# Where a mixer's small products accumulate: the projections' two PSUM banks, or first the weighed values' two

## The chip, the cores and the metric

One core of a Trainium2 chip runs the whole program. The metric is the device time of one execution in microseconds (us), the median of several runs. The core has a matrix engine (TensorE, PE in the profile, with its weight loads as PEld), a vector engine (DVE), a scalar engine (ACT), GpSimd (POOL), a queue engine for transfers (SP), and an accumulator memory (PSUM) of eight banks into which all matrix products go. Each engine takes its instructions strictly in the order in which the program holds them: an instruction that waits holds up all behind it on that engine.

## The reference

Two layers of a decoder trunk over 512 tokens and 16 meta tokens (528 positions), 1024 channels, float32. Each layer is a mixer and a feed-forward part. The mixer is what the change touches:

```python
u = rms_norm(h, pre_g)
z = jnp.einsum("bld,de->ble", u, w_in)
q, k, v, f_logit, a_val, a_gate, sc_b, sc_c, sc_x = jnp.split(z, idx, axis=-1)
...
y_attn = forgetting_attention(q, k, v, log_f)       # 8 heads of 64
a = a_val * jax.nn.sigmoid(a_gate)
a = causal_depthwise_conv(a, a_dw_w) + a_dw_b       # 31 taps, 256 channels
a = jax.nn.silu(layer_norm(a, a_ln_g, a_ln_b))
y_conv = jnp.einsum("blc,ce->ble", a, a_pw_w)       # the pointwise product
y_sc = sc_b * causal_depthwise_conv(sc_c * sc_x, sc_conv_w)
y = jnp.concatenate([y_attn, y_conv, y_sc], axis=-1)
y = jnp.einsum("ble,ed->bld", head_rms_norm(y, head_g), w_out)
return h + rms_norm(y, post_g)
```

`head_rms_norm` scales each group of 64 channels by the inverse root of its mean square. Then the feed-forward part: `w_up` to 5632 channels, a 3-tap convolution, `silu(g) * up`, `w_down`.

## The kernel before

Activations lie with channels on the 128 partitions and positions along the row, 528 of them in two halves of 264 (`H`). Every float32 product is made of three fast ones from values split into a high and a low part (`mm3`, line 671): high by high, low by high, high by low. The weights come in blocks of 128x1024; ACT rounds a block to its high part (line 625 in the planned stages), DVE subtracts for its low part (line 629).

The order of the work in a mixer is written by a planner, `Flow`. Each piece of PE work is a generator ("thread"): `fill` runs the projections one after the other, `maxima` the row maxima of each head's logits (lines 1402 and 1426), `exponentials` the logits again and their exponentials (line 1448), `weighing` the products of the exponentials with the values and their sums for a pair of heads (line 1494), `att_norms` the mean squares of a finished pair (line 1560). The convolution branch runs as `conv_tail`: the means for its layer norm (line 1578), the mean squares (line 1607), then the pointwise product; its two outputs and the two of the short convolution go through `plain_head_norm` (line 1176). The planner holds a clock for each engine with an estimated duration for each instruction, and each time it lets go on whatever could start first. What comes out of it is a fixed order of instructions on each engine; on the chip, semaphores make each instruction wait for its inputs and for its bank, whatever the planner believed.

A product may only be planned once it holds a bank. In a mixer the eight banks are four rings of two: `mm` (0, 1) for projections, `s1` (3, 4) for maxima, attention's head norms and the gate, `st` (5, 6) for logits, `acc` (2, 7) for the weighed values and their sums. A ring hands out its oldest bank, and only once the planner's clock has passed the time at which that bank's last reader ends. A projection holds a bank of `mm` through 24 matmuls and its eviction. Before the change, the layer norm's means and mean squares, the pointwise product's four halves and the plain head norms take theirs from `mm` too; so `mm` serves the projections and the convolution branch in turn. `weighing` takes both banks of `acc` and one of `s1` at once for each of the four pairs of heads.

One half of a head norm is: a matmul with `bd` on PE (the mean squares in PSUM, line 1176 or 1560), logarithm, exponential and square on ACT (lines 1141, 1144, 1145), two combining steps on DVE (1146, which reads PSUM and frees the bank, and 1149), the scaling on DVE (1160), the rounding on ACT (1163) and the low part on DVE (1164). The intermediate tiles `rs_r` and `rs_t` are two of each, so two halves can be under way at once.

When `maxima` and `fill` have ended, `Early` starts the first two columns of `w_out` on the banks of the projections: for each finished input block `k` (0 to 3 attention, 4 and 5 convolution, 6 and 7 short convolution) and half, six matmuls, in the order in which the planner expects the blocks to be normed. Those six need the block's high and low parts, the outputs of lines 1163 and 1164. So the last head norms of a mixer stand between the last projections and the rest of `w_out`.

Of the kernel before, what the change touches and what calls it, by code (L numbers as in the profile page):

```python
# [208 lines left out]
class Flow:  # L209
# [32 lines left out]
    def thread(self, gen, first=False):  # L242
        self.threads.insert(0 if first else len(self.threads), [gen, [Tok(self.pe)]])

    def grab(self, ring, slot=None):

        while True:
            t = ring.slots[0].time
            if t is not None and t <= self.pe:
                slot = slot or Slot()  # L250
                ring.take(slot)
                return slot
            yield [Head(ring)]

    @staticmethod
    def ready(waits, least=0.0):
# [56 lines left out]
def mm_us(n, k=P):  # L313

    return max(n / 2400 + 0.012, 0.00086 * k)


def act_us(n):
    return 0.17 + 0.0009 * n


def dve_us(n):
    return 0.17 + 0.00101 * n


def stt_us(n):
    return 0.22 + 0.00102 * n
# [13 lines left out]
def tile_hybrid_trunk(ctx: ExitStack, tc: tile.TileContext, xT, wflat, pv_d, out):  # L341
# [4 lines left out]
    def T(pool, shape, dt, tag, bufs=None):  # L346
        uid[0] += 1
        kw = {} if bufs is None else {"bufs": bufs}
        return pool.tile(list(shape), dt, tag=tag, name=f"{tag}_{uid[0]}", **kw)
# [18 lines left out]
    def mmt(i=None):  # L368

        if i is None:  # L370
            i = PAIRS[n_pairs[0] % 2]
            n_pairs[0] += 1
        return psum[:, i:i + 2]
# [46 lines left out]
    flow = Flow()  # L420
# [6 lines left out]
    def half_sl(hf):  # L427
        return slice(H * hf, H * (hf + 1))
# [87 lines left out]
    def act(us, fn, *after, **kw):  # L516
        return flow.op("act", us, fn, after, **kw)

    def dve(us, fn, *after, **kw):
        return flow.op("dve", us, fn, after, **kw)  # L520
# [144 lines left out]
    def mm3(dst, w, ks, rhs, start=True, stop=True, cols=slice(None)):  # L665

        n = len(ks)
        for i, k in enumerate(ks):
            for p, (a, b) in enumerate(((0, 0), (0, 1), (1, 0))):
                for hf, d in dst.items():  # L670
                    nc.tensor.matmul(d, lhsT=w[a][:, k, cols],  # L671
                                     rhs=rhs(b, k, hf),
                                     start=start and i == 0 and p == 0,
                                     stop=stop and i == n - 1 and p == 2)
# [284 lines left out]
    def mixer(l, ypool, first, close_first, spans, front, rz0_at):  # L959
        pv, pg = pvs[l]  # L960

        def col(name, j):
            return pv[:, _COLS[name] + j:_COLS[name] + j + 1]

        def gcol(name, j):
            return pg[:, _COLS[name] + j:_COLS[name] + j + 1]
# [138 lines left out]
        banks = {"mm": Ring((0, 1)), "s1": Ring((3, 4)), "st": Ring((5, 6)), "acc": Ring((2, 7))}  # L1105
        rings = {"p": Ring(NPT), "rs": Ring(2)}

        def bank(kind):

            slot = yield from flow.grab(banks[kind])  # L1110
            return psum[:, slot.buf], slot

        def proj(use):
# [16 lines left out]
        def ytiles(i):  # L1130
            return (T(ypool, [P, L], F32R, f"yhi{i}"), T(ypool, [P, L], F32R, f"ylo{i}"))
# [21 lines left out]
        def head_norm(i, yt, hf, x, slot, eps, tok):  # L1153

            if hf == 0:
                y[i] = ytiles(i)
            yhi, ylo = y[i]
            c = half_sl(hf)
            box, mine, e = rsq(x, slot, eps, tok)
            f = dve(stt_us(H), lambda: nc.vector.scalar_tensor_tensor(  # L1160
                yt[:, c], in0=yt[:, c], scalar=gcol("head_g", i), in1=box["t"], op0=ALU.mult, op1=ALU.mult), e)
            mine.close(f)
            g = act(act_us(H), lambda: nc.scalar.copy(yhi[:, c], yt[:, c]), f)  # L1163
            d = dve(dve_us(H), lambda: nc.vector.tensor_sub(ylo[:, c], yt[:, c], yhi[:, c].bitcast(F32)), g)  # L1164
            y_at[i, hf] = [g, d]
            return d

        def plain_head_norm(i, yt, sq, toks, waits=()):

            sqs = [act(act_us(H), lambda hf=hf: nc.scalar.activation(sq[:, half_sl(hf)], yt[:, half_sl(hf)], AF.Square),  # L1170
                       toks[hf], *waits) for hf in range(2)]
            out = []
            for hf in range(2):
                yield [sqs[hf]]
                ps, slot = yield from bank("mm")
                nc.tensor.matmul(ps[:, :H], lhsT=bd, rhs=sq[:, half_sl(hf)], start=True, stop=True)
                out.append(head_norm(i, yt, hf, ps[:, :H], slot, RMS_EPS, flow.mm(4 * mm_us(H))))
                yield
            return out

        def sc_norm(j):
            sq = T(mq, [P, L + 2], F32, "cxp")[:, :L]
            yield from plain_head_norm(6 + j, sc[j], sq, [sc_at[j, "b", hf] for hf in range(2)])
            sc_done[j] = True
# [381 lines left out]
        def conv_tail(blk):  # L1566

            w = blk.w
            yield taps
            a2 = [ytiles(4), ytiles(5)]  # L1570
            sq = [T(mq, [P, L + CK - 1], F32, "apad", 2) for _ in range(2)]
            us, vs = act_us(H), dve_us(H)
            at = {}
            for hf in range(2):
                c = half_sl(hf)
                ps, slot = yield from bank("mm")
                for j in range(2):
                    nc.tensor.matmul(ps[:, :H], lhsT=om_c, rhs=conv[j][:, c], start=j == 0, stop=j == 1)
                tok = flow.mm(8 * mm_us(H))
                subs = []  # L1580
                for j in range(2):
                    subs.append(dve(vs, lambda j=j, ps=ps, c=c: nc.vector.tensor_sub(
                        conv[j][:, c], conv[j][:, c], ps[:, :H]), tok))
                    at[hf, j] = act(us, lambda j=j, c=c: nc.scalar.activation(sq[j][:, c], conv[j][:, c], AF.Square), subs[-1])
                slot.close(*subs)
                yield
            done = {}

            def silu(j, c, box, mine, e):
                n, s = conv[j][:, c], sq[j][:, c]  # L1590
                f = dve(stt_us(H), lambda: nc.vector.scalar_tensor_tensor(
                    n, in0=n, scalar=gcol("a_ln_g", j), in1=box["t"], op0=ALU.mult, op1=ALU.mult), e)
                mine.use(f)
                f = dve(vs, lambda: nc.vector.tensor_scalar(n, in0=n, scalar1=col("a_ln_b", j), scalar2=None, op0=ALU.add), f)
                g = act(us, lambda: nc.scalar.activation(s, n, AF.Exp, scale=-1.0), f)
                g = act(us, lambda: nc.scalar.activation(s, s, AF.Ln, bias=c_one), g)
                g = act(us, lambda: nc.scalar.activation(s, s, AF.Exp, scale=-1.0), g)
                f = dve(vs, lambda: nc.vector.tensor_mul(n, n, s), g)
                g = act(us, lambda: nc.scalar.copy(a2[j][0][:, c], n), f)
                return dve(vs, lambda: nc.vector.tensor_sub(a2[j][1][:, c], n, a2[j][0][:, c].bitcast(F32)), g)  # L1600

            for hf in range(2):
                c = half_sl(hf)
                yield [at[hf, 0], at[hf, 1]]
                ps, slot = yield from bank("mm")
                for j in range(2):
                    nc.tensor.matmul(ps[:, :H], lhsT=om_c, rhs=sq[j][:, c], start=j == 0, stop=j == 1)
                box, mine, e = rsq(ps[:, :H], slot, LN_EPS, flow.mm(8 * mm_us(H)))
                done[hf] = [silu(j, c, box, mine, e) for j in range(2)]
                mine.close()  # L1610
                yield
            yts, got = [], {}
            ends = done[0] + done[1]
            for m in range(2):
                yield ends
                yt = T(mq, [P, L], F32, "cacc", 2)
                for hf in range(2):
                    ps, slot = yield from bank("mm")
                    mm3({hf: ps[:, :H]}, w, range(2), lambda b, k, hf: a2[k][b][:, half_sl(hf)],
                        cols=slice(P * m, P * (m + 1)))  # L1620
                    tok = flow.mm(6 * mm_us(H))
                    got[m, hf] = act(us, lambda ps=ps, yt=yt, hf=hf: nc.scalar.copy(yt[:, half_sl(hf)], ps[:, :H]), tok)
                    slot.close(got[m, hf])
                    yield
                yts.append(yt)
            blk.slot.close(tok)
            for m in range(2):
                sq = T(mq, [P, L + CK - 1], F32, "apad", 2)[:, :L]
                flow.thread(plain_head_norm(4 + m, yts[m], sq, [got[m, hf] for hf in range(2)]), True)
# [261 lines left out]
    for l in range(DEPTH):  # L1891
# [21 lines left out]
        with tc.tile_pool(name=f"fp{l}", bufs=2, reuse_waits="tile") as fp:  # L1913
# [78 lines left out]
            for part, nf in enumerate(PARTS):  # L1992
                for f in range(f0, f0 + nf):
                    for i in (2 * f, 2 * f + 1):
# [6 lines left out]
                        ps = mmt()  # L2001
# [5 lines left out]
                if part < len(PARTS) - 1:  # L2007
                    for m in range(KD):
                        w = next_w()
                        ps = mmt()  # L2010
# [76 lines left out]
```

## Time and profile before

| | |
|---|---|
| time, median of 3 runs | 1301.84 us (1299.65 to 1301.91) |
| the profiled execution's own time | 1300.12 us |
| its span, first to last instruction | 1298.4 us |
| PE busy | 1271.5 us, 98% of the span |
| DVE, ACT, POOL busy | 894.8, 612.8, 110.2 us |
| mixer of layer 0, about | 45 to 222 us of the span |
| mixer of layer 1, about | 665 to 866 us |

The profile is one execution. Busy time is the union of an engine's instructions. Matmuls overlap each other, so PE counts as busy for a little longer than it computes; what counts for the path is the time from one matmul's start to the next one's. "Idle before" is time in which an engine had nothing under way before an instruction, with what ended it. PEclk is the share of full clock that the throttle granted to PE.

### The profile page before, as it was taken

What the parts mean: (1) busy time and instruction counts of PE and PEld (TensorE: products, weight loads), DVE (VectorE), ACT (ScalarE), POOL (GpSimd) and SP (SyncE); (2) the same over time, 40 slices, a digit from 0 to 9 for tenths busy, and PEclk for the clock granted to TensorE, in tenths of its full rate; (3) what the DMA queues carried; (4) which work ended last, traced back from release to release, by engine and by line L of the source; (5) the groups of instructions that cost most, each with busy time, mean ns of one, the idle gap of its engine ahead of it and who ended that gap; (6) DMA issues with size and microseconds to landing.
All of it is one profiled execution on the core that took longest, in us unless ns stands there. A gap on an engine that the chain in (4) does not pass through costs nothing. (4 is left out here: it accounts for less than half of the span.)

```text
span 1298.4 us, 24320 instructions
## 1 busy us (share of the span) xinstructions
PE 1271.5 (98%) x9922; PEld 1216.3 (94%) x9922; DVE 894.8 (69%) x1563; ACT 612.8 (47%) x1144; POOL 110.2 (8%) x270
## 2 busy tenths in 40 slices
PE   8999999999999999999999999989999999999997
PEld 7989978999999999999999898889999799989997
DVE  7888896688734775677568886756876256636664
ACT  7255568655433442444562445666543234314443
POOL 1311210100000000000203222100000000000000
PEclk9999999999999999999999999999999999999999
DMA  6133123515644556754542453414032222232321
GB/s 222 50 101 80 45 83 100 182 63 200 223 159 158 202 176 235 237 201 145 214 158 98 118 163 122 129 63 147 22 96 96 97 86 92 72 119 89 92 72 65
DMA packets 55440, 164.57 MB, mean 127 GB/s; under 512 B 6352, under 2 KB 16720, under 8 KB 55328
## 3 DMA queue, kind: packets, MB, share of 16 engines
q1 hardware_dynamic: 41200, 109.56, 25.5%
q0 software_dynamic: 14128, 53.45, 12.8%
q8 instruction: 78, 1.28, 0.4%
q14 instruction: 34, 0.28, 0.1%
HBM read 131.17 MB, written 27.46 MB: 122 GB/s over the span
## 5 line engine op out<-in xcount | busy, mean ns | idle before, releaser
L671 PE MATMUL psum<-uhi,whi 128*128 128x264 f32 (+1 forms) x1936 | 452.2, 287 | 1.0 <-ACT uhi L1865 0.9
L671 PE MATMUL psum<-ulo,whi 128*128 128x264 f32 (+1 forms) x1936 | 445.1, 284 | 0.5 <-DVE ulo L1867 0.4
L671 PE MATMUL psum<-uhi,wlo 128*128 128x264 f32 (+1 forms) x1936 | 444.7, 283 | 0.0
L671 PEld LDWEIGHTS psum<-uhi,whi 128*128 128x128 f32 x1936 | 322.5, 188 | 3.2 <-ACT uhi L1865 1.1
L671 PEld LDWEIGHTS psum<-ulo,whi 128*128 128x128 f32 x1936 | 322.1, 188 | 1.8 <-DVE ulo L902 0.6
L671 PEld LDWEIGHTS psum<-uhi,wlo 128*128 128x128 f32 x1936 | 322.3, 189 | 0.0
L671 PE MATMUL psum<-yhi,whi 128*128 128x264 f32 (+3 forms) x888 | 250.3, 305 | 6.7 <-ACT whi L625 2.2
L671 PE MATMUL psum<-yhi,wlo 128*128 128x264 f32 (+3 forms) x888 | 247.2, 300 | 0.9 <-DVE wlo L629 0.7
L671 PE MATMUL psum<-ylo,whi 128*128 128x264 f32 (+3 forms) x888 | 247.0, 300 | 0.6 <-DVE ylo L1164 0.5
L476 ACT CAST whi<-raw 128x1024 fp32r<-128x1024 f32 (+1 forms) x110 | 113.1, 1030 | 184.6 <-PE psum L671 146.1
L477 DVE TENSOR_TENSOR wlo<-raw,whi 128x1024 fp32r<-128x1024 f32 (+1 forms) x110 | 131.7, 1199 | 65.0 <-ACT whi L476 63.3
L671 PEld LDWEIGHTS psum<-yhi,whi 128*128 128x128 f32 x888 | 160.4, 190 | 14.6 <-ACT yhi L1163 2.6
L671 PEld LDWEIGHTS psum<-ylo,whi 128*128 128x128 f32 x888 | 160.6, 190 | 7.0 <-DVE ylo L1164 1.3
L671 PEld LDWEIGHTS psum<-yhi,wlo 128*128 128x128 f32 x888 | 160.8, 190 | 6.6 <-DVE wlo L629 1.3
L1968 DVE SCALAR_TENSOR_TENSOR c<-z,pv,c 128x528 f32<-128x528 f32 (+1 forms) x176 | 131.9, 756 | 2.7
L617 POOL DMA_DIRECT2D raw<-in_w_dram x60 | 32.1, 535 | 922.2 <-DVE wlo L477 703.9
L629 DVE TENSOR_TENSOR wlo<-raw,whi 128x1024 fp32r<-128x1024 f32 (+2 forms) x64 | 75.7, 1197 | 30.9 <-ACT whi L625 30.5
L987 DVE SCALAR_TENSOR_TENSOR cacc<-apad,pv,cacc 128x528 f32<-128x528 f32 x120 | 87.5, 763 | 0.9
L625 ACT CAST whi<-raw 128x1024 fp32r<-128x1024 f32 (+2 forms) x64 | 64.6, 1028 | 30.7 <-PE psum L671 16.0
L1978 ACT ACTIVATE c<-c 128x528 f32<-128x528 f32 (+1 forms) x44 | 28.1, 639 | 84.0 <-DVE c L1968 84.0
L1986 ACT CAST yhi<-c 128x528 fp32r<-128x528 f32 (+1 forms) x44 | 27.5, 625 | 84.4 <-DVE c L1982 84.2
L1966 ACT ACTIVATE c<-z,pv 128x528 f32<-128x528 f32 (+1 forms) x88 | 63.4, 727 | 0.1
(223 smaller groups left out, 1473.1 us busy)
## 6 DMA issues: line engine op xcount, KB each, us to landing
raw<-in_w_dram SPq DMA_DIRECT2D x116, 512.0 KB
raw<-in_w_dram POOLq DMA_DIRECT2D x44, 512.0 KB, 4.3
split_w<-whi SPq DMA_DIRECT2D x20, 512.0 KB
split_w<-wlo SPq DMA_DIRECT2D x20, 512.0 KB
whi<-split_w POOLq DMA_DIRECT2D x20, 512.0 KB, 4.7
wlo<-split_w POOLq DMA_DIRECT2D x20, 512.0 KB, 6.2
raw<-in_w_dram SPq DMA_DIRECT2D x20, 448.0 KB
raw<-in_w_dram POOLq DMA_DIRECT2D x12, 448.0 KB, 3.6
```

The source lines that it names most:

```text
L476: nc.scalar.copy(hi[:, :sz], raw[:, :sz])
L477: nc.vector.tensor_sub(lo[:, :sz], raw[:, :sz], hi[:, :sz].bitcast(F32))
L617: nc.gpsimd.dma_start(to, src)
L625: nc.scalar.copy(box["hi"][:, :sz], box["raw"][:, :sz])
L629: nc.vector.tensor_sub(lo[:, :sz], box["raw"][:, :sz], box["hi"][:, :sz].bitcast(F32))
L671: nc.tensor.matmul(d, lhsT=w[a][:, k, cols], rhs=rhs(b, k, hf), start=start and i == 0 and p == 0, stop=stop and i == n - 1 and p == 2)
L987: nc.vector.scalar_tensor_tensor(conv[j], in0=src, in1=conv[j], scalar=col("a_dw_w", CK * j + i), op0=ALU.mult, op1=ALU.add)
L1966: nc.scalar.activation(dst, src[:, 2:2 + 2 * fw], AF.Copy, scale=wtap(2, t))
L1968: nc.vector.scalar_tensor_tensor(dst, in0=src[:, i:i + 2 * fw], scalar=wtap(i, t), in1=dst, op0=ALU.mult, op1=ALU.add)
L1978: silu = nc.scalar.activation(cs[0], cs[0], AF.Silu)
L1986: nc.scalar.copy(ghi, cs[0])
```

## The change

`grab`, which gives a thread its bank, may now be given several rings: it takes from the first ring whose oldest bank is free, and else waits for the soonest. Four places are changed to ask `acc` first and `mm` second: the layer norm's means, its mean squares, the pointwise product, and the plain head norms. Nothing is computed differently, and the number of instructions is the same. Every line after the first hunk is one higher in the changed file.

```diff
-    def grab(self, ring, slot=None):
+    def grab(self, ring, slot=None, *more):
         while True:
-            t = ring.slots[0].time
-            if t is not None and t <= self.pe:
-                slot = slot or Slot()
-                ring.take(slot)
-                return slot
-            yield [Head(ring)]
+            for r in (ring, *more):
+                t = r.slots[0].time
+                if t is not None and t <= self.pe:
+                    slot = slot or Slot()
+                    r.take(slot)
+                    return slot
+            yield [Soonest([Head(r) for r in (ring, *more)])]
...
-        def bank(kind):
-            slot = yield from flow.grab(banks[kind])
+        def bank(kind, *more):
+            slot = yield from flow.grab(banks[kind], None, *(banks[k] for k in more))
             return psum[:, slot.buf], slot
...
# plain_head_norm, the layer norm's means, its mean squares, the pointwise product: each
-                ps, slot = yield from bank("mm")
+                ps, slot = yield from bank("acc","mm")
```

The planner makes another order of it, in both mixers, from the first plain head norm (short convolution, block 6) to the last one. Outside the mixers the order is the same. Three places on PE follow. In the rows, `uhi` and `ulo` are the normed input's parts and `whi`, `wlo` a weight block's: with them a row is a projection. Numbers tell buffers apart.

PE in the mixer of layer 1, the last head's maxima: the last product of queries and keys (line 1402), the transposing of the maxima (`mcol`, line 1426) and the first logits that use them (1448). Before:

```order
L1402 MATMUL psum_67<-k_764_7985,q_772_7993 128x264
L1448 MATMUL psum_67<-q_770_7991,k_762_7983 16x16
L1448 MATMUL psum_67<-q_771_7992,k_763_7984 16x16
L1402 MATMUL psum_67<-k_764_7985,q_772_7993 128x264
L1426 MATMUL psum_67<-ident_r_76,mcol_9554 1x16
L1426 MATMUL psum_67<-ident_r_76,mcol_9554 1x128 x4
L1448 MATMUL psum_67<-q_772_7993,k_764_7985 128x16
L1448 MATMUL psum_67<-q_773_7994,k_765_7986 128x16
```

Of the change, from the same product on, with the projection's matmuls that now stand between:

```order
L1449 MATMUL psum_67<-q_770_7991,k_762_7983 128x144
L1449 MATMUL psum_67<-q_771_7992,k_763_7984 128x144
L1427 MATMUL psum_67<-ident_r_76,mcol_9561 1x16
L1427 MATMUL psum_67<-ident_r_76,mcol_9561 1x128 x3
L1449 MATMUL psum_67<-q_770_7991,k_762_7983 16x16
L1449 MATMUL psum_67<-q_771_7992,k_763_7984 16x16
L672 MATMUL psum_67<-uhi_106,whi_9382 128x264
L672 MATMUL psum_67<-ulo_107,whi_9382 128x264
L672 MATMUL psum_67<-uhi_106,wlo_9383 128x264
...
L1427 MATMUL psum_67<-ident_r_76,mcol_9561 1x128
```

Nine projection matmuls now stand between the two pieces of line 1426, six more before the first logits, and six before the last product of 1402; before there were none. In layer 0 the same head gets three between and nine after.

PE in layer 1, the pointwise product (`pw` is its weight) after the last pair's mean squares (line 1560). Before:

```order
L1560 MATMUL psum_67<-sq_9701,bd_93 128x264 x2
L671 MATMUL psum_67<-uhi_106,whi_9446 128x264
L671 MATMUL psum_67<-ulo_107,whi_9446 128x264
L671 MATMUL psum_67<-uhi_106,wlo_9447 128x264
...
L671 MATMUL psum_67<-yhi_899_9533,pw_9348 128x264
L671 MATMUL psum_67<-ylo_900_9534,pw_9348 128x264
```

Of the change:

```order
L1561 MATMUL psum_67<-sq_9739,bd_93 128x264 x2
L672 MATMUL psum_67<-uhi_106,whi_9448 128x264
L672 MATMUL psum_67<-ulo_107,whi_9448 128x264
L672 MATMUL psum_67<-uhi_106,wlo_9449 128x264
...
L672 MATMUL psum_67<-yhi_899_9533,pw_9343 128x264
L672 MATMUL psum_67<-ylo_900_9534,pw_9343 128x264
```

The left-out rows are the same projection's: 24 of its matmuls stood between the two, now 6. In layer 0 the four halves of this product, which were spread over the projections' last rows and `Early`, now stand together, 24 rows in a piece.

PE in layer 0, the last plain head norms (line 1176) and the `w_out` products that wait for them: `yhi_292` and `yhi_294` were blocks 5 and 4. Before:

```order
L1176 MATMUL psum_67<-apad_2668,bd_93 128x264
L671 MATMUL psum_67<-yhi_283_2593,whi_2430 128x264
L671 MATMUL psum_67<-ylo_284_2594,whi_2430 128x264
L671 MATMUL psum_67<-yhi_283_2593,wlo_2467 128x264
L1176 MATMUL psum_67<-apad_2667,bd_93 128x264
L671 MATMUL psum_67<-yhi_292_2678,whi_2239 128x264
L671 MATMUL psum_67<-ylo_293_2679,whi_2239 128x264
```

Of the change, the last two plain head norms (blocks 7 and 5) and what follows; `yhi_273` and the rows after it are block 3, ready since long, `yhi_284` is block 4:

```order
L1177 MATMUL psum_67<-cxp_2596,bd_93 128x264
L1177 MATMUL psum_67<-apad_2590,bd_93 128x264
...
L672 MATMUL psum_67<-yhi_273_2532,whi_2250 128x264
L672 MATMUL psum_67<-ylo_274_2533,whi_2250 128x264
L672 MATMUL psum_67<-yhi_273_2532,wlo_2282 128x264
L672 MATMUL psum_67<-yhi_284_2603,whi_2250 128x264
L672 MATMUL psum_67<-ylo_285_2604,whi_2250 128x264
```

Before, layer 0 had 18 of `Early`'s matmuls between the last norm's matmul (block 4, second half) and the first that needs this norm, and 15 for the norm ahead of it (block 5, second half); now the last one is block 5's second half, and 57 matmuls stand between. In layer 1 it was 24 and is 63. The first four norms of the tail now follow each other on PE almost at once (three `apad`, one `cxp` in layer 0). One new place without cover arises: in layer 0 the maxima of head 3 now stand with the five rows of line 1426 followed by line 1448 at once, where 12 projection matmuls stood between.

More of the change, by code (lines that the diff above doesn't have):

```diff
@@ L1575, in conv_tail @@
                 c = half_sl(hf)
-                ps, slot = yield from bank("mm")
+                ps, slot = yield from bank("acc","mm")
                 for j in range(2):
@@ L1604, in conv_tail @@
                 yield [at[hf, 0], at[hf, 1]]
-                ps, slot = yield from bank("mm")
+                ps, slot = yield from bank("acc","mm")
                 for j in range(2):
@@ L1617, in conv_tail @@
                 for hf in range(2):
-                    ps, slot = yield from bank("mm")
+                    ps, slot = yield from bank("acc","mm")
                     mm3({hf: ps[:, :H]}, w, range(2), lambda b, k, hf: a2[k][b][:, half_sl(hf)],
```

## The prediction

> **What bounds the kernel now.** I read the page first, then the busy time by stretches, then PE's waits in the two mixers, and last the order of time around the long ones.
>
> ```profile
> PE 1271.5 (98%) x9922; PEld 1216.3 (94%) x9922; DVE 894.8 (69%) x1563; ACT 612.8 (47%) x1144; POOL 110.2 (8%) x270
> ...
> 150.00:200.00 50.00, 48.47 (x387) 42.34 (x386) 44.80 (x113) 32.91 (x86) 8.74 (x23) 1.00 0.32 100
> 200.00:250.00 50.00, 48.05 (x365) 46.81 (x364) 28.63 (x49) 33.39 (x70) 5.54 (x14) 0.97 0.41 134
> 350.00:400.00 50.00, 50.00 (x412) 50.00 (x412) 19.41 (x21) 17.88 (x24) 0.00 (x0) 1.00 0.45 149
> ```
>
> After a stretch's length stand the busy times of PE, PEld, DVE, ACT and POOL, then the granted clock. PE is the bound nearly everywhere: in the feed-forward stretch it runs 412 matmuls in 50 us, 0.121 us each, with nothing to gain. The change removes no matmul, so all it can win or lose is time in which PE stands still, and the clock. Such time lies in the mixers. Here are PE's waits from 75 to 228 us (layer 0, from the first reordered row on) and from 714 to 870 (layer 1), the last three numbers being us in total, times, longest:
>
> ```profile
> PE psum L671 <- ACT yhi L1163: 1.5, 1, 1.5
> PE psum L1448 <- ACT q L1429: 0.8, 1, 0.8
> PE psum L1402 <- DMA k<-sq: 0.5, 1, 0.5
> PE psum L1448 <- ACT p L1457: 0.5, 1, 0.5
> PE psum L671 <- DVE ylo L1164: 0.5, 2, 0.3
> PE psum L1426 <- DVE mcol L1409: 0.3, 1, 0.3
> PE psum L1402 <- DVE rs_t L1146: 0.3, 1, 0.3
> PE psum L1402 <- DVE mcol L1409: 0.2, 1, 0.2
> ...
> PE psum L671 <- DVE sccx L1088: 2.5, 1, 2.5
> PE psum L1448 <- ACT q L1429: 1.1, 2, 0.9
> PE psum L1426 <- DVE mcol L1409: 0.7, 2, 0.5
> PE psum L671 <- ACT yhi L1163: 0.7, 1, 0.7
> PE psum L671 <- ACT acc L759: 0.5, 1, 0.5
> ```
>
> That is 4.6 us and 5.5 us. On top comes the clock. It fell to half after two of these stalls, and not after the longest:
>
> ```profile
> 220.00:225.00 5.00, 4.46 (x22) 4.24 (x22) 1.40 (x4) 3.82 (x9) 0.27 (x4) 0.66 0.00 0
> 825.00:829.00 4.00, 3.80 (x12) 3.12 (x12) 2.94 (x9) 1.82 (x6) 0.31 (x1) 0.57 0.00 0
> 843.00:847.00 4.00, 1.50 (x13) 1.32 (x12) 3.67 (x10) 1.20 (x3) 0.00 (x0) 1.00 0.54 157
> ```
>
> At a mean clock of 0.66 over 5 us, 0.34 x 5 = 1.7 us of work were lost; at 0.57 over 4 us again 1.7 us. So what the mixers could give back at most is 4.6 + 5.5 + 3.4 = 13.5 us.
>
> **The change part by part.** First the wait that it is about. PE's row and DVE's rows around 843 us, and ACT's last read of the weighed values:
>
> ```profile
> 837.59 0.61 ACT L1525 COPY yta<-psum 128x512 f32<-128x512 f32 x1
> 842.03 0.76 DVE L1067 SCALAR_TENSOR_TENSOR sccx<-cxp,pv,sccx 128x528 f32<-128x528 f32 x1
> 844.88 0.76 DVE L1067 SCALAR_TENSOR_TENSOR sccx<-cxp,pv,sccx 128x528 f32<-128x528 f32 x1
> 845.90 0.42 DVE L1088 TENSOR_TENSOR sccx<-psum,sccx 128x264 f32<-128x264 f32 x1
> 846.47 0.36 PE L671 MATMUL psum<-yhi,pw 128*128 128x264 f32 x1 [2.50 <-DVE sccx L1088]
> ```
>
> The pointwise product wanted a projections' bank that a short convolution's eviction (L1088) was to free, and that stood on DVE behind two late taps (L1067) and head-norm steps. The weighed values' banks had been read out at 838.2, over 5 us before. With the change the first two halves go there. Their inputs are ready in time: the low parts (L1600 on DVE) need not wait for L1088, and 6 projection matmuls and the pair's mean squares stand ahead. **2.5 us** gone. The eviction of the product (ACT L1622) now has to free a bank for the fourth half within the time of the third; ACT has head-norm steps queued ahead of it. Bounds: nothing, or two such steps at the 0.61 us of the copy above, which is wider than they are, 1.2; I take **0.5 us** lost, in both layers together.
>
> Second, the last head's maxima. Here before, in layer 1:
>
> ```profile
> 824.20 0.44 PE L1426 MATMUL psum<-ident_r,mcol 16*1 16x16 f32 x4 [0.52 <-DVE mcol L1409]
> 824.85 0.22 PE L1426 MATMUL psum<-ident_r,mcol 128*1 128x128 f32 x1 [0.21 <-DVE mcol L1409]
> 825.27 1.58 PE L1448 MATMUL psum<-q,k 128*128 128x16 f32 x4 [0.20 <-ACT q L1429]
> ```
>
> It is a chain PE, DVE, PE, ACT, PE with nothing between. With the change nine and six projection matmuls (15 x 0.121 = 1.8 us) stand in it in layer 1, three and nine (1.5 us) in layer 0; the idle pieces to be covered are 0.52 + 0.21 + 0.20 here, and 0.3 + 0.8 in layer 0. Layer 1's other wait for ACT q, 0.9 us (head 1), gets six matmuls more as well, 0.7 us, and layer 0's 0.2 us before a line 1402 gets longer cover. So of the rows for mcol and ACT q, 0.8 + 0.3 + 0.2 + 1.1 + 0.7 = **3.1 us** go. Against it, head 3 of layer 0 now has line 1426 followed by line 1448 at once: the same arrangement cost 0.8 us there for head 7, so **0.8 us** lost.
>
> Third, the tail. The group of a weight block's rounding, and the last two head norms of layer 0, before:
>
> ```profile
> L625 ACT CAST whi<-raw 128x1024 fp32r<-128x1024 f32 (+2 forms) x64 | 64.6, 1028 | 30.7 <-PE psum L671 16.0
> ...
> 216.16 0.61 PE L1176 MATMUL psum<-apad,bd 128*128 128x264 f32 x2
> 217.32 0.47 ACT L1141 ACTIVATE rs_r<-psum,c_rms 128x264 f32<-128x264 f32 x1
> 220.16 0.49 DVE L1160 SCALAR_TENSOR_TENSOR cacc<-cacc,pg,rs_t 128x264 f32<-128x264 f32 x1
> 220.28 0.51 PE L671 MATMUL psum<-yhi,whi 128*128 128x264 f32 x2 [1.47 <-ACT yhi L1163]
> 220.57 0.99 DVE L1164 TENSOR_TENSOR ylo<-cacc,yhi 128x264 fp32r<-128x264 f32 x2
> ```
>
> From the matmul (216.16) to the low part (221.56) a norm takes 5.4 us; 15 and 18 matmuls (about 2 us) covered it. Now 57 stand there in layer 0 (6.9 us) and 63 in layer 1 (7.6 us), above 5.4. So the waits for yhi and ylo in both layers go, 1.5 + 0.5 + 0.7 = **2.7 us**. But the norms now come in a bunch, and only two can be under way at once, since `rs_r` and `rs_t` are two of each: a pair holds them from its first L1141 to its last L1160, 217.32 to 220.65, 3.3 us. Three pairs in a row from the first bunched matmuls on need 3 x 3.3 + 0.9 to round and split the last = 10.8 us; PE has 30 matmuls, two norms' own and 57 more, 87 x 0.121 = 10.5 us and 2 x 0.61, so 11.7. That is 0.9 us to spare, and a weight block's rounding on ACT (1.03 us, L625) stands between. I take **1.0 us** lost in layer 0; in layer 1, with its first norms spread by `Early`'s rows, **0.5**. Bounds: nothing, or 4.2 us a pair (first L1141 to the last low part, 217.32 to 221.56): 3 x 4.2 = 12.6 and that block's 1.0 against 11.7, 1.9 us, in each layer.
>
> Fourth, small ones. The waits for ACT p (0.5) and DVE rs_t (0.3) fall where the order has been drawn apart: **0.8 us** gone. The 0.5 us for ACT acc L759 at the end of layer 1 stays in part, since the last block's halves now end 12 matmuls apart and not 6: **0.2** gone. The DMA's 0.5 stays. In layer 0 the mean squares of the layer norm now follow the means with 1.8 us of cover; in layer 1 before it was 1.9 us and showed no wait: **0.3** lost. `exponentials` of head 3 is packed as densely as where ACT p cost 0.5: **0.4** lost.
>
> Fifth, the clock. With the stalls at 218 and 822 gone, their dips go: **3.4 us**, bounds nothing and 3.4. [...]
>
> Last, waits at places I cannot name. Everything in both mixers moves by some rows, so each of the many handovers that are now just covered may be just missed. The rows of before hold five waits of 0.2 to 0.3 us besides the long ones; I allow twice their sum, **2.0 us**, with bounds of nothing and 5.
>
> The sum: 2.5 + 3.1 + 2.7 + 0.8 + 0.2 + 3.4 = 12.7 us gone; 0.5 + 0.8 + 1.5 + 0.3 + 0.4 + 2.0 = 5.5 us new. Net 7.2 us. From the profiled execution's own 1300.12 us that gives 1292.9, and I say **1293 us**. The median shown is 1301.84, so the profiled execution was a fast one of its kind, but inside the range of the runs (from 1299.65); I leave the sum as it is.
>
> **The rivals.** [...]
>
> *A new order, the same waits.* The planner knows nothing of real lateness: DVE is busy 44.8 of 50 us from 150 to 200, and where it is late in the old order it will be late elsewhere in the new. Then about 10 us of waits and one dip of 1.7 us return: 1300.1 - 1.7 = 1298.4, or with both dips 1300.1; I put it at 1299.5. Against: the long waits stood in chains with no cover at all, and those have cover now.
>
> *Slower: weighing held up by its own banks.* `weighing` needs both `acc` banks, and now sums stand in them before pair 0 and pair 3 in each layer. A sum's bank is free once DVE has done L1146. Before, from the matmul to L1146's end:
>
> ```profile
> 736.22 0.71 PE L1176 MATMUL psum<-cxp,bd 128*128 128x264 f32 x2
> 740.46 0.43 DVE L1146 SCALAR_TENSOR_TENSOR rs_t<-psum,rs_t 128x264 f32<-128x264 f32 x1
> ```
>
> 4.7 us with the wait in DVE's queue. By the order there are now, between the last sum and pair 3 in layer 1, 30 projection matmuls (3.6 us) and ten of logits, which I put at two of those each (2.4), so 6 us of PE's work; before the other three weighings it is about 2 us more. It decides once DVE takes longer than that; behind the weighing then stands all of PE. If each hold grew to 10 us, 4 + 3 x 2 = 10 us would be lost, and two dips: 1293 + 10 + 3.4 = 1306.4. Against: it takes twice the lateness seen. That the change does nothing is excluded by the order.
>
> **How the numbers follow.** The forecast has a chance of 0.50, the dips 0.15, the same waits 0.23, the held weighing 0.12. Faster or slower means by more than 0.2%, 2.6 us, about what a measurement of this kernel can tell: under 1299.2 or over 1304.4. Forecast and dips are faster, 0.65; of the same waits 0.06 is faster, 0.14 the same, 0.03 slower; of the held weighing 0.10 slower, 0.02 the same. Faster 0.71, same 0.16, slower 0.13. The range goes from all that can go with little new (1300.1 - 12.7 = 1287.4, so 1287.5) up to the same waits and a little above, 1303.
>
> **What would show it.** In the changed profile no PE wait for DVE sccx L1088 (one line lower there, as all), none over 0.5 us for yhi before `Early`'s last blocks, waits for mcol and ACT q under 1.5 us in all, granted clock 1.00 from 216 to 226 and from 820 to 850; one new wait of about 0.8 us near layer 0's head 3. PE waits in both mixers should sum to 5 or 6 us. Wrong it would be if rows like "L1494 <- DVE rs_t" appear (the held weighing), or if waits of over 1 us stand in new places.

## The result, and the profile after

The changed kernel takes **1291.47 us**, the median of four runs (1291.14 to 1293.17); the kernel before, beside it, 1301.78 (1299.65 to 1301.91). The ratio is 0.9927, 95% interval 0.991 to 0.9944: about 10 us or 0.7% faster. The prediction was 1293 us, within 1287.5 to 1303. The profiled execution took 1291.36 us with a span of 1289.7, 8.7 under the 1298.4 of before. The medians lie further apart, since the profiled execution of before, 1300.12 us, was 1.7 us quicker than its median; what follows accounts for the 8.7.

The busy times of the whole span, of the changed kernel:

```profile
PE 1268.0 (98%) x9922; PEld 1217.2 (94%) x9922; DVE 894.8 (69%) x1563; ACT 611.3 (47%) x1144; POOL 111.8 (9%) x270
```

The same 9922 matmuls, and DVE, ACT and POOL as busy as before, within about 2 us. PE is busy 3.5 us less, so of the 8.7 us of span the other 5.2 are idle time. By the first matmul of the stage behind each mixer (line 808, now 809) the mixer of layer 0 ends at 248.20 us instead of 250.13, and layer 1's at 885.00 instead of 893.75. The stages between the two take 387.1 us in both. So up to the end of layer 0's mixer the change gave 1.9 us (2.2 from the first reordered row, at 88 us, which the changed kernel reaches 0.3 us later), layer 1's mixer gave 6.8, and the rest of the kernel nothing.

PE's waits in the changed kernel, from 75 to 228 us (layer 0) and then from 712 to 862 (layer 1); us in total, times, longest:

```profile
PE psum L672 <- ACT yhi L1164: 2.0, 1, 2.0
PE psum L1449 <- ACT q L1430: 1.0, 1, 1.0
PE psum L1403 <- DMA k<-sq: 0.4, 1, 0.4
PE psum L672 <- ACT acc L760: 0.4, 1, 0.4
PE psum L1449 <- ACT p L1458: 0.2, 1, 0.2
...
PE psum L672 <- ACT yhi L1164: 1.6, 1, 1.6
PE psum L1561 <- DVE sq L1527: 0.2, 1, 0.2
```

4.0 and 1.8 us, where 4.6 and 5.5 stood. Gone are the 2.5 us for the short convolution's eviction (`sccx`, now L1089), every wait for `mcol` and, but for one, those for `q`. Left is one stall at head 3 of layer 0, and one in each tail, for the last head norms' high part. The clock, after a stretch's length and the busy times of PE, PEld, DVE, ACT and POOL:

```profile
217.00:227.00 10.00, 7.63 (x57) 6.82 (x56) 6.27 (x11) 6.81 (x13) 1.32 (x6) 1.00 0.05 7
820.00:850.00 30.00, 30.00 (x243) 27.42 (x243) 23.88 (x60) 24.99 (x72) 3.63 (x11) 1.00 0.30 101
122.00:132.00 10.00, 8.88 (x58) 8.05 (x57) 7.67 (x24) 4.38 (x11) 3.52 (x9) 0.83 0.40 121
852.00:862.00 10.00, 8.43 (x56) 8.06 (x56) 4.82 (x11) 7.64 (x18) 0.00 (x0) 0.83 0.01 4
```

The two places that had lost clock before have it whole now, and from 820 to 850 us PE is never idle. But head 3 and layer 1's tail lose 0.17 x 10 = 1.7 us each. In the mixers of these two executions there are two dips before (from 221.21 and 825.37 us) and two after (from 126.50 and 856.95 us).

Now the tail of layer 0, PE first, then ACT in order of time:

```profile
216.97 0.28 PE L672 MATMUL psum<-yhi,wlo 128*128 128x264 f32 x1
219.26 0.51 PE L672 MATMUL psum<-yhi,whi 128*128 128x264 f32 x2 [2.00 <-ACT yhi L1164]
...
210.43 0.47 ACT L1142 ACTIVATE rs_r<-psum,c_rms 128x264 f32<-128x264 f32 x1
211.11 0.48 ACT L1142 ACTIVATE rs_r<-psum,c_rms 128x264 f32<-128x264 f32 x1
...
214.46 0.41 ACT L1164 CAST yhi<-cacc 128x264 fp32r<-128x264 f32 x1 [1.62 <-DVE cacc L1161]
214.78 0.47 ACT L1142 ACTIVATE rs_r<-psum,c_rms 128x264 f32<-128x264 f32 x1
215.15 0.40 ACT L1164 CAST yhi<-sccx 128x264 fp32r<-128x264 f32 x1
215.45 0.48 ACT L1142 ACTIVATE rs_r<-psum,c_rms 128x264 f32<-128x264 f32 x1
...
218.79 0.41 ACT L1164 CAST yhi<-sccx 128x264 fp32r<-128x264 f32 x1 [1.61 <-DVE sccx L1161]
```

The norms' matmuls are over at 210.7 us (216.4 before), yet the last high part is only begun at 219.20 (220.7 before). Pairs start at 210.43 and 214.78: 4.35 us a pair. ACT stands idle 1.6 us per pair, for DVE's scaling (L1161), with the next pair's first step queued right behind the rounding that waits.

### The profile page after: what moved, and what is told of

Same layout as the page of the kernel before. It is cut to its first block, busy times and chain, and to the rows that moved or that the text cites. A ratio compares the mean times of both kernels' runs of the same rounds, so it can differ in the third digit from the quotient of the medians.

```text
span 1289.7 us, 24331 instructions
## 1 busy us (share of the span) xinstructions
PE 1268.0 (98%) x9922; PEld 1217.2 (94%) x9922; DVE 894.8 (69%) x1563; ACT 611.3 (47%) x1144; POOL 111.8 (9%) x270
```

## The experiments

**One kind of work at a time.** Three kernels: `grab` and `bank` as changed, but only one of the kinds asks `acc` before `mm`. The pointwise product alone:

```diff
                 for ...:   # the pointwise product
-                    ps, slot = yield from bank("mm")
+                    ps, slot = yield from bank("acc","mm")
```

> Before, with the pointwise product alone allowed to take the weighed values' banks first; layer norm sums and plain head norms stay on the projections' two. Theory (each part removes the waits that stood on its own bank): the 2.5 us wait for DVE sccx L1088 in layer 1 goes; the last head's maxima in both layers, their clock dip and layer 0's tail wait stay. About 1299 us, 2 to 3.5 us under before. Rival (the gain came from the new order as such, not from the banks): then any of the reordered kernels may land anywhere between 1291 and 1303, with waits in other places.

Measured 1298.79 us, ratio 0.9975 (0.996 to 0.999): 3.3 us faster than the 1302.05 of before in the same set. PE's longest waits in layer 1, 714 to 870 us:

```profile
PE psum L1449 <- ACT q L1430: 1.1, 2, 0.9
PE psum L672 <- ACT yhi L1164: 0.9, 1, 0.9
PE psum L1427 <- DVE mcol L1410: 0.7, 2, 0.5
```

The 2.5 us are gone, and none of the others. This wait was the bank's, as the prediction read it. The rest of the 3.3 us is less sure. The eight runs spread from 1296.28 to 1301.71 us, with mean granted clocks from 0.997 to 0.991, and the profiled one, the fastest, at 0.997, has no dip behind head 7's stall in layer 1, though the stall itself stayed: a dip that is lost or gained, 3.41 us at half clock, moves such a run by 1.7 us.

The plain head norms alone (only the line at 1176 asks for `acc` first):

> Before, with the plain head norms alone allowed the weighed values' banks. Theory: layer 0's head 3 then has the new uncovered chain (a wait of about 1 us for ACT q) as in the change, the last head's maxima stay uncovered in both layers, and the 2.5 us wait for sccx L1088 stays or moves, since the pointwise product still takes a projections' bank; layer 1's head 1 wait of 0.9 us goes. About 1300 us, within 2 us of before. Rival (new order as such): as low as the whole change, 1291 to 1295.

Measured 1296.7 us, ratio 0.9956 (0.9943 to 0.9969), 5.4 us faster: a miss, the largest single part and not the smallest. Its longest waits in layer 0, 75 to 228 us, and in layer 1:

```profile
PE psum L1449 <- ACT q L1430: 1.1, 2, 1.0
PE psum L672 <- ACT acc L760: 0.5, 1, 0.5
PE psum L672 <- ACT yhi L1164: 0.4, 1, 0.4
PE psum L672 <- DVE ylo L1165: 0.3, 1, 0.3
...
PE psum L672 <- DVE sccx L1089: 2.5, 1, 2.5
PE psum L1427 <- DVE mcol L1410: 0.7, 2, 0.5
```

The tails are nearly clean here: 0.4 + 0.3 us for high and low parts in layer 0, none in layer 1. The norms come earlier, but spread (their matmuls run from 203.6 to 212.3 us, in the whole change from 204.6 to 210.7). The stall at head 3 belongs to this part. Here too the profiled execution, at a mean granted clock of 0.996, has no dip behind head 7's stall in layer 1, though the waits for `mcol` stayed.

The layer norm's means and mean squares alone (lines 1577 and 1606 of the changed file):

> Before, with the layer norm's means and mean squares alone allowed the weighed values' banks. Theory: the last head's maxima get projection matmuls in between in both layers, so 1.1 us (layer 0) and 0.9 us (layer 1) of waits and the clock dip at 825 us (1.7 us) go; layer 0's tail wait and its dip stay; the 2.5 us wait for sccx L1088 may stay. About 1297.5 us. Together the three single parts should come near the whole change's 10 us: 2.5 to 3.5, 0 to 2 and 4 to 5. Rival (new order as such): the three singles do not add up to the whole at all.

Measured 1298.77 us, ratio 0.9973 (0.9964 to 0.9982), 3.3 us faster, 1.3 us less than I expected. Head 7's chain has no wait in either layer. The one for `sccx` is gone too: the short convolution's eviction now comes at 842.10 us, before the pointwise product starts at 843.76. This kernel's tail in layer 0, 205 to 225 us, is worse than before:

```profile
PE psum L672 <- ACT yhi L1164: 3.6, 3, 2.2
PE psum L1177 <- DVE rs_t L1147: 0.9, 2, 0.5
```

There the plain norms still take turns with the projections in `mm`. The parts sum to 3.3 + 5.4 + 3.3 = 12.0 us, the whole gives 10.3. Two of them remove the same 2.5 us, which would leave 9.5. The intervals of the parts are 1.2 to 2.0 us wide to each side, so the sum tells nothing finer; the split that I had expected between them (0 to 2 for the norms, 4 to 5 for the layer norm) was wrong.

**Which ring first.** The change, but the four places ask `mm` first and `acc` second:

```diff
-                ps, slot = yield from bank("acc","mm")
+                ps, slot = yield from bank("mm","acc")
```

> The change with the two rings in the other order: all four uses ask the projections' two banks first and the weighed values' two second. Theory (what counts is that a second pair of banks may be had, not which is asked first): the gain stays, 1289 to 1294 us, without a wait for sccx L1088 and with the last head's maxima covered; by its order layer 0's head 3 has cover again, so the wait of 1.0 us there and the clock dip after it, 1.7 us, may go: 1289. Rival (the projections must be kept free of the small products): projections wait for their banks again, 1296 to 1300.

Measured 1292.71 us, ratio 0.9925 (0.9908 to 0.9943): against its before as good as the change. PE's waits above 0.3 us are these, in layer 0 and layer 1:

```profile
PE psum L672 <- ACT yhi L1164: 1.6, 1, 1.6
PE psum L1449 <- ACT p L1458: 0.4, 1, 0.4
...
PE psum L672 <- ACT yhi L1164: 1.6, 1, 1.6
```

Head 3's stall and dip are gone (the granted clock is 1.00 from 123 to 131 us), the tails stay and both have a dip (0.83 from 214 to 224 us, 0.87 from 850 to 862). So what pays is the leave to take a second pair of banks; which pair is asked first changes which places are left bare, and the time by no more than the noise.

**The tails' two tiles.** The change, with three tiles of `rs_r` and `rs_t` instead of two, so three halves of a head norm can be under way:

```diff
-        rings = {"p": Ring(NPT), "rs": Ring(2)}
+        rings = {"p": Ring(NPT), "rs": Ring(3)}
...
-                box["r"], box["t"] = (T(mp, [P, H], F32, f"rs_{i}", 2) for i in "rt")
+                box["r"], box["t"] = (T(mp, [P, H], F32, f"rs_{i}", 3) for i in "rt")
```

> The change with three instead of two of the intermediate tiles rs_r and rs_t for the mixers' norms; the order is the same up to the last norms. Theory (at the tail, two tiles let the norms go only in pairs of 4.3 us each, which is why PE still waits 2.0 us in layer 0 and 1.6 us in layer 1 for yhi, with a clock dip in layer 1): both waits fall to under 0.7 us and the dip at 857 us goes: 3 to 5 us under the change, 1286.5 to 1288.5. Rival (ACT and DVE have no more to give there, the pairs are their pace): the waits stay, within 1 us of the change.

And the same two lines on the kernel before:

> The kernel before with three instead of two of rs_r and rs_t. Theory: the tail waits (1.5 + 0.5 us in layer 0, 0.7 us in layer 1) shrink by half or more, and with them perhaps the dip at 221 us (1.7 us); the other waits stay: 1298 to 1300.5. Rival (the late banks, not the tiles, set the old tail): within 1 us of before.

With the change 1289.18 us (1288.4 to 1290.45), ratio 0.9907 (0.989 to 0.9923), about 2.3 us under the change alone; without it 1301.14, ratio 1.0 (0.9991 to 1.0009). Both missed what I expected, 1286.5 to 1288.5 and 1298 to 1300.5. The tails with the change and three tiles, PE's longest wait from 205 to 225 and from 845 to 865 us, and two of ACT's rows:

```profile
PE psum L672 <- DVE ylo L1165: 0.5, 1, 0.5
...
PE psum L672 <- DVE ylo L1165: 0.3, 1, 0.3
...
208.26 0.85 ACT L1142 ACTIVATE rs_r<-psum,c_rms 128x264 f32<-128x264 f32 x2
208.99 1.06 ACT L1145 ACTIVATE rs_r<-rs_r 128x264 f32<-128x264 f32 x3
```

Steps now run three at a time, no wait for `yhi` is left, and layer 1's dip is gone (1.00 from 850 to 862 us). So the two tiles set the new tail. In the old tail they cost something too, by the trace of the kernel before with three tiles (layer 0, 205 to 225 us; in layer 1 no such wait is left):

```profile
PE psum L671 <- ACT yhi L1163: 0.9, 2, 0.7
...
PE psum L671 <- DVE ylo L1164: 0.3, 1, 0.3
```

In both layers together these waits fell from 2.7 us to 1.2, by more than half as the theory had it, and the dips at 221 and 825 us are absent, the second though its stall stayed. But the time is the rival's: 1301.14 against 1301.53, no change clear of noise. Two things in the trace work against it, a new wait of 0.5 us for ACT `acc` in layer 0 and a dip behind the wait for `sccx`, which had none before (its rows stand at the end); whether they explain all of it is open.

**Is it only the shuffle?** Any change of the planner moves every row a little. As a control I shifted the order without touching the banks: in the mixers the planner's allowance between engines (`HOP`) is 0.09 us instead of 0.06, once on the kernel before and once on the change.

```diff
             flow.yields = YM
+            flow.HOP = 0.09
             y, y_at, early = mixer(l, ypool, first, wxs.close, i_spans, front, rz0_at)
         ms, front = ExitStack(), None
+        flow.HOP = 0.06
```

> A control: the kernel before, banks as before, with the planner's allowance for a handover between engines at 0.09 instead of 0.06 us inside the mixers. It puts the mixers' instructions in another order and does nothing else. Theory (the gain comes from the banks): the last head's maxima have no cover again by its order (layer 0 wholly, layer 1 in part), so the time stays within 4 us of before, 1298 to 1305. Rival (another order as such is worth as much): 1291 to 1295.

> The same control on the change: banks as changed, the planner's allowance at 0.09 instead of 0.06 us inside the mixers. Theory: the gain stays whatever the order's details, 1289 to 1296 us; layer 0's head 3 is uncovered here too (about 1 us, perhaps with a dip). Rival (the gain was the luck of one order): 1297 to 1303.

Before with the shift: 1301.53 us, ratio 0.9998 (0.9989 to 1.0008). The change with the shift: 1293.88, ratio 0.9945 (0.993 to 0.996). In layer 1 the shifted kernel before waits elsewhere, and for no less, 6.5 us in all the waits listed against 5.5; its longest:

```profile
PE psum L671 <- ACT yhi L1163: 1.5, 1, 1.5
PE psum L671 <- DVE rs_t L1146: 1.3, 2, 0.9
PE psum L671 <- DVE wlo L629: 1.1, 1, 1.1
```

That is the rival "a new order, the same waits" as it looks when it happens: no time won. With the banks the gain outlives the shift, less some 2 us. It outlives it in layer 1 alone, though. From the end of layer 0's mixer to the end of layer 1's the kernel before takes 643.6 us and the change 636.8; shifted they take 643.8 and 636.7. But from one row that all four share, at about 45 us, to the end of layer 0's mixer it is 205.5 and 203.1, and shifted 206.2 and 206.2: there the shifted change has head 3 bare, as expected, waits of 3.3 us for `yhi` and a dip in the tail, from 218.75 us. So layer 0's gain hangs on the order.

**Both edits that helped.** `mm` asked first, and three tiles:

> The change with both of the single edits that helped: the four kinds ask for the projections' banks first ("mm", "acc"), and there are three rs_r and rs_t tiles. Theory (what the change still loses are two separate things: the bare chain of head 3 in layer 0, 0.95 us and the dip behind it, which goes when the norms next to it ask for mm first; and the pairs of norms in the two tails, which go with three tiles): no PE wait for ACT q at head 3, no yhi wait above 0.6 us in either tail, no clock dip inside the mixers, and the time 2 to 3 us under the three tiles alone (1289.18), 1286.5 to 1288. Rival (the two orders' gains are the same stall time, moved about; what is saved in one place comes back in another): 1289 to 1291, with a stall of over 0.9 us or a dip somewhere in the mixers.

Measured 1288.56 us (1288.2 to 1289.68), ratio 0.9903 (0.9886 to 0.9919). The clock around head 3 and the two tails:

```profile
121.00:135.00 14.00, 13.97 (x118) 13.33 (x116) 11.64 (x32) 6.93 (x18) 2.73 (x7) 1.00 0.33 100
210.00:225.00 15.00, 14.13 (x106) 13.04 (x104) 11.05 (x22) 10.94 (x25) 1.86 (x7) 1.00 0.16 49
845.00:862.00 17.00, 16.14 (x125) 15.03 (x124) 13.19 (x28) 12.31 (x27) 1.59 (x3) 1.00 0.14 40
```

No stall above 0.6 us and no dip in the mixers, as I expected. But the time did not come down by the 2 to 3 us that went with it. To the end of layer 0's mixer this kernel is 2.84 us ahead of the change with three tiles alone, by its profile, but 1.3 of that it has already at 76 us, where the two still run the same rows; in layer 1 it gives 1.1 back, of which only a 0.3 us wait for ACT `p` shows. In the medians 0.6 us are left, and the ranges of the two overlap. It has the lowest median of all, 13 us under the kernel before, but that it beats `acc` first with three tiles is not shown.

## Why the prediction came out as it did

The number was right to 1.5 us, and partly by luck: the two largest errors in it were made good by others. The gain that it forecast was 7.2 us; between the profiled executions it is 8.8, between the medians 10.3. Its terms, against the rows of the changed kernel:

| step of the prediction | said, us | found |
|---|---|---|
| wait for `sccx` L1088 | -2.5 | -2.5 |
| waits for `mcol` and `q` | -3.1 | -3.1 |
| ACT `p`, DVE `rs_t` | -0.8 | -0.8 |
| ACT `acc` | -0.2 | -0.1: from 0.5 in layer 1 to 0.4 in layer 0 |
| waits for `yhi`, `ylo` in the tails, with the pairs' price | -2.7 + 1.5 | +0.9: from 2.7 to 3.6 |
| DMA's wait | 0 | -0.1 |
| two clock dips | -3.4 | 0: two others, in this execution |
| head 3 of layer 0 bare | +0.8 | +1.0 |
| product's eviction, mean squares | +0.5, +0.3 | none |
| `exponentials` of head 3 | +0.4 | +0.2 |
| places not named | +2.0 | +0.2 (`sq`) |

**The chains.** The two readings on which the forecast rested held row by row: PE stood behind a bank that DVE freed late, and the last head's maxima stood with no work beside them. The first is shown by the pointwise product alone. The second: with the layer norm alone changed head 7's waits go in both layers, with the whole change no wait for `mcol` is left, and the new stall came where it was foreseen:

```profile
124.76 0.96 PE L1449 MATMUL psum<-q,k 128*128 128x16 f32 x4 [0.95 <-ACT q L1430]
```

**The tails: the step that failed was the price of a pair.** I saw that two tiles allow two norms at once, and took 3.3 us a pair, "from its first L1141 to its last L1160, 217.32 to 220.65". But these two rows belong to one norm, the last. The other norm of that pair had begun before it:

```profile
216.19 0.47 ACT L1141 ACTIVATE rs_r<-psum,c_rms 128x264 f32<-128x264 f32 x1
```

So that pair held the two tiles from 216.19 to 220.65, 4.46 us. In the changed kernel the pair that starts at 210.43 ends with these steps:

```profile
213.93 0.49 DVE L1161 SCALAR_TENSOR_TENSOR cacc<-cacc,pg,rs_t 128x264 f32<-128x264 f32 x1
214.34 0.49 DVE L1161 SCALAR_TENSOR_TENSOR sccx<-sccx,pg,rs_t 128x264 f32<-128x264 f32 x1
```

It holds them to 214.83, 4.40 us. The first tile is free at 214.42 and the next pair's first step starts at 214.78, behind a rounding in ACT's queue; so the queue adds a little, and the hold itself is the most of the 4.35. Layer 1's tail has the same pitch (847.35 to 851.70). The upper bound of 4.2 that stood beside the 3.3 came near it by luck, since it was read off the same single norm, to its low part. By that bound, 1.9 us a layer, the tails would have cost 3.8; the two waits for `yhi` are 3.6. That the tiles are what held them is shown by the third one.

**The clock: the term of 3.4 us failed.** That the stalls at 218 and 822 us would go, and their dips with them, was right; that no new one would come was not, in the execution profiled: two came, at 126.50 and 856.95 us, by the head-3 stall and the tail that the prediction itself had listed. It gave such dips a chance of 0.15. What decides how many an execution has was not shown; the last section has what was measured.

**What made it good.** Clock and pairs were 3.4 + 2.1 us too good. The allowances for evictions, mean squares, exponentials and unnamed places were 2.8 too dear, head 3's 0.2 too cheap. By waits alone the gain would thus be 10.1 - 5.8 = 4.3 us, as the rows say. The other 4.4 us are not in the waits listed: PE's busy time fell by 3.5, and the rest is idle time too short for the list. I had priced a stall at the idle time that the row shows. Here is what stood around head 7's chain in layer 1 before the change:

```profile
823.29 0.39 PE L1402 MATMUL psum<-k,q 128*128 128x264 f32 x1
824.20 0.44 PE L1426 MATMUL psum<-ident_r,mcol 16*1 16x16 f32 x4 [0.52 <-DVE mcol L1409]
```

From 823.29 to 824.20 one matmul starts: 0.91 us where such a one usually takes 0.12 (412 in 50 us in the feed-forward stretch, 0.121 each). Of the 0.79 us lost the row shows 0.52, since the matmul before counts as busy to its end, at 823.68. Counted like this for every row, from its start to the next one's less the median for such rows in all the traces, the chain from 822.3 to 828.8 us lost 3.8 us, 1.5 of it at half clock, where its rows show 0.93; after the change 0.2 are left there. Layer 0's chain lost 1.9 against 1.15. Layer 1's gain then comes to 2.7 for `sccx`, 1.1 for head 1 and 3.6 for head 7, less 1.1 for the tail, which lost 2.5 before and loses 3.6 now: 6.3 of the 6.8 us measured. This sum is worked out from the starts; no run tested it by itself.

**The rivals.** Weighing held by its banks did not come: no row of line 1495 waits. "The same waits" is excluded for the whole by the result and the control; in layer 0 the shifted change is a case of it. **What would show it** held on `sccx`, `mcol` and `q` (1.0 us in all), on the clock at the two old places, on head 3 and on the total, 5.8. It failed on "none over 0.5 us for yhi before `Early`'s last blocks" and on "waits of over 1 us in new places": both are the tails' 2.0 and 1.6.

## What to carry to other kernels

When the bound engine waits for a buffer, look for another pool that lies idle at that moment and let the planner take from either; here the leave mattered, and the preference moved the bare places. After a queue is fed sooner, price its next limit for all that share its buffers, from the first one's first step to the last one's last: here 4.4 us for a pair and not the 3.3 of one norm, and a third tile brought 2.3 us more. Price a stall from start to start, and try a shift of the order that changes nothing else before a gain is put down to a mechanism.

## What the runs showed of the hardware

Each of the four dips inside the mixers of the two kernels lasted 3.41 us at a granted clock of 0.50: from 221.21 and 825.37 us before, from 126.50 and 856.95 us after. The two of one trace start 604.16 us and 730.45 us apart, 177 and 214 times 3.4133 us. In the 3.41 us ahead of each, PE was busy in part only, 1.68 and 2.35 us before, 2.29 and 1.84 after, with 11 and 16, 16 and 14 matmuls; from 839.02 us of before, where nothing held it up, 27 ran in 3.42 us. In the kernel before, the stretch ahead of the second dip and the dip, then two stretches of the same length around the `sccx` wait:

```profile
821.96:825.37 3.41, 2.35 (x16) 1.40 (x14) 3.02 (x11) 2.79 (x9) 1.24 (x4) 1.00 0.42 154
825.37:828.78 3.41, 3.41 (x10) 2.80 (x11) 2.57 (x8) 1.23 (x5) 0.31 (x1) 0.50 0.00 0
842.44:845.85 3.41, 1.53 (x13) 1.32 (x11) 3.41 (x9) 1.26 (x4) 0.17 (x1) 1.00 0.79 241
845.85:849.26 3.41, 2.79 (x23) 2.82 (x24) 0.81 (x3) 1.40 (x5) 0.00 (x0) 1.00 0.00 1
```

The same `sccx` wait, in the kernel before with three tiles:

```profile
841.52:844.94 3.42, 0.96 (x8) 0.75 (x7) 3.42 (x10) 1.20 (x3) 0.00 (x0) 1.00 1.07 369
844.94:848.35 3.41, 3.36 (x15) 3.39 (x16) 0.24 (x1) 0.72 (x2) 0.00 (x0) 0.50 0.16 65
```

No dip came with that wait of 2.5 us where it left 13 matmuls in the one stretch and 23 in the next, and none with the head norms alone changed, where 15, 21 and 26 ran in the three stretches from 837.69 us, all at 1.00. A dip came where 8 were left in one stretch. But 16, small ones among them, stood ahead of the dip at 825.37 us, and after the 17 from 215.25 us in the changed kernel, with PE busy for 2.00 us, the clock stayed at 1.00. So neither the length of a wait nor the number of matmuls alone tells here whether a dip follows. That it matters where a stall falls is my estimate from these rows; no run tested it.

Nor do the dips come at the same place: counted from the first instruction, the first dip inside a mixer comes 2.76 us past a multiple of 3.4133 us before and 0.21 after. It comes at 2.37 with the pointwise product alone and at 1.85 before with three tiles, though all these run the same rows up to 76 us. No kernel has a second trace here, so how far the dips of one kernel move from one execution to the next was not shown.
